# ConvGLU on one core: a looser order for the weight splits of the column tiles, and a second seven-product tile in the tenth group

## The chip, the cores and the metric

The kernel is one program on one core of a Trainium2 chip. The metric is the device time of one execution in microseconds (us); lower is better. The engines are named as in the profile: PE is the matrix engine, PEld its weight loads, DVE the vector engine, ACT the scalar engine, POOL the third elementwise engine (here it only issues DMAs), SP the queue that issues most DMAs.

## The reference, cut to what matters

A decoder block with d_model 2048 and 256 tokens: token mixers, cross-attention, and at the end a ConvGLU feed-forward of width 5632. All is float32. The change lies in the first half of the feed-forward:

```python
def conv_glu_ffn(u, w_up, conv_w, conv_b, w_down):
    gate, up = jnp.split(u @ w_up, 2, axis=-1)
    gate = causal_dwconv(gate, conv_w, conv_b)
    return (jax.nn.gelu(gate, approximate=False) * up) @ w_down
```

## The kernel before, in words

**Products in parts.** Each float32 weight tile (1 MB, 128 x 2048) is fetched by SP into a buffer named `raw` (three of them) and split into a rounded part `hi` and a remainder `lo`: ACT casts (L142), DVE subtracts (L143), in two halves of 1024 columns. `hi` and `lo` have five buffers each, so a half can only be split when the PE has let go of the half five places earlier. PE multiplies hi by hi, hi by lo and lo by hi.

**The feed-forward.** The 5632 channels are 44 chunks of 128. The first 40 go in ten groups (`FG = 10`, loop variable `p`) of four chunks. A group is eight weight tiles. An ordinary tile is 24 matmuls of 512 columns. A tile "by seven products" replaces the eight block products by seven (a Strassen-Winograd form): 21 matmuls, but DVE first makes four sums of weights (L183, 512 columns each), and the seven forms are split by ACT (L177) and DVE (L178) in three casts of 1024 columns and one of 512. `up_steps` says which tiles are so made: in groups 1 to 9 the fourth and the sixth, in group 10 the fourth alone.

The last four chunks go as eight **column tiles** (gate and up for each chunk, `for c in range(4 * FG, KF)`): a tile is 16 matmuls of 512 columns and 16 of 256, its result is joined by an ACT copy (`jt`, L290) and a DVE addition (L291). Every second column tile multiplies the `lo` halves first. After them comes the down projection, 2 x 22 tiles, of which 14 are by seven products with sums of the activations as inputs (`input_forms`, into `xs`, which the order calls `s2`).

**Work beside.** When a group's products are done, `taken_up` adds, scales and transposes the results (DVE L1227, ACT L1229, DVE L1230), POOL sends them through memory, and `four` does the convolution, gelu and product of the group's four chunks some tiles later (ACT L1189, L1164, L1184, L305; DVE L1167, L1185, L306). These steps are generators in `background`; each call of `weights()` runs one step of each and then prefetches: it issues the splits of the weight tile two ahead.

**What sets the order.** Each engine works its queue in order, and a scheduler lays the queues at build time, unless told that one instruction is to be issued after another (`issue_after`). From group 1 to the last column tile `state["strict"]` is on, and `weights()` gives two such rules: the step's instructions go after the `hi` and `lo` of the next tile, and the splits that are issued with the step go after all of the step's DVE and ACT instructions (`queued`).

Of the kernel before, what the change touches and what calls it, by code (L numbers as in the profile page):

```python
# [44 lines left out]
FG = 10  # L45


def up_steps(p):
    sevens = {3: 0, 5: 1} if p < FG - 1 else {3: 0}
    rest = [q for q in range(KD // 2) if q not in sevens.values()]  # L50
    return [(True, sevens[j]) if j in sevens else (False, rest.pop(0)) for j in range(KD // 2)]

# [20 lines left out]
def hybrid_trunk(ctx, tc, xT, memT, par, cst, msk, w_k0, w_ka, w_va, w_hg, w_hv, w_hog, w_ghg, w_bhg, w_dt,  # L73
                 w_z, w_m2, w_gm2, w_bm2, w_out, w_q, w_o, w_up, w_ut, w_dn, fin_g, outT):
    nc = tc.nc
    V, S, G, PE = nc.vector, nc.scalar, nc.gpsimd, nc.tensor
# [18 lines left out]
    order = [w_ka[n] for n in range(KD - NS)]  # L95
# [17 lines left out]
    for p in range(FG):  # L113
        for i, (seven, _) in enumerate(up_steps(p)):
            if seven:
                sums.add(len(order))
            order.append(w_up[p, i])
# [4 lines left out]
    AHEAD = 2  # L122
    WB = 5
    ready, lows = [], {}
    state = {"issued": 0, "used": 0, "strict": False}

    def halves(w, c, d, table=None):

# [69 lines left out]
    def step():  # L198
        pin.append(True)
        for gen in list(background):  # L200
            if next(gen, False) is False:
                background.remove(gen)
        pin.pop()

    def drain():
        while background:
            step()
# [5 lines left out]
    def prefetch(ahead):  # L213
        while state["issued"] < min(state["used"] + ahead, len(order)):
            issue()

    def weights():
        with ExitStack() as queued:
            if state["strict"]:
                traced = nc.cur_bb.bb.instructions  # L220
                n = len(traced)
                high, low = lows[state["used"] + 1]
                with tc.issue_after(high.ins), tc.issue_after(low.ins):
                    step()
                for ins in traced[n:]:
                    if ins.engine in (V.engine, S.engine):
                        queued.enter_context(tc.issue_after(ins))
            else:
                step()
            prefetch(1 + AHEAD)  # L230
        state["used"] += 1
        parts = ready.pop(0)
        return parts if state["used"] - 1 in sums else viewer(parts)

    def viewer(parts):
        def view(j, width):
            for a, b, hi, lo in parts:
                if a <= j * width < b:
                    o = j * width - a
                    return hi[:, o:o + width], lo[:, o:o + width]  # L240

        return view
# [22 lines left out]
    def project(hl):  # L265
        w = weights()
        ps = pj.tile([P, 512], F32, name="proj")

        mm_run(ps, w, [(k, hl[:, k, :]) for k in range(KD)], True, True, state["used"] % 2 == 0)
        return ps  # L270

    def project_tok(hl):

        ps = [pj.tile([P, 512], F32, name="proj") for _ in range(2)]
        for i in range(4):
            w = weights()
            for j in range(4):
                k = 4 * i + j
                wh, wl = w(j, 512)
                for g in range(2):  # L280
                    x1 = hl[:, k, g * P:(g + 1) * P]
                    x2 = hl[:, k, T + g * P:T + (g + 1) * P]
                    mm(ps[g], lhsT=x1, rhs=wh, start=(k == 0), stop=False)
                    mm(ps[g], lhsT=x1, rhs=wl, start=False, stop=False)
                    mm(ps[g], lhsT=x2, rhs=wh, start=False, stop=(k == KD - 1))
        return ps

    def join(pool, ps, out):
        tmp = pool.tile([P, T], F32, name="jt", bufs=2)
        S.copy(out=tmp, in_=ps[:, T:2 * T])  # L290
        V.tensor_tensor(out=out, in0=ps[:, 0:T], in1=tmp, op=ALU.add)  # L291
# [12 lines left out]
    def split(dst, src):  # L304
        S.copy(out=dst[..., 0:T], in_=src)  # L305
        V.tensor_tensor(out=dst[..., T:2 * T], in0=src, in1=dst[..., 0:T].bitcast(F32), op=ALU.subtract)  # L306
# [658 lines left out]
    for i in range(4):  # L965
        w = weights()
        ks = range(i // 2 * 8, i // 2 * 8 + 8)
        for j in range(2):
            hl_run(pss[i % 2 * 2 + j], [(*w(8 * j + k - ks[0], P), mg[:, k, :]) for k in ks],
                   i < 2, i >= 2)  # L970
# [190 lines left out]
    def convolved(c, g, taken=None):  # L1161

        gc = fu.tile([P, T], F32, name="gc", bufs=2)
        S.activation(out=gc if taken is None else token_order(gc), in_=g if taken is None else taken,  # L1164
                     func=AF.Identity, bias=pc("f_cb", c), scale=pc("f_cw", 3 * c + 2))
        for s in range(1, 3):
            V.scalar_tensor_tensor(out=gc[:, s:T], in0=g[:, 0:T - s],  # L1167
                                   scalar=pc("f_cw", 3 * c + 2 - s), in1=gc[:, s:T],
                                   op0=ALU.mult, op1=ALU.add)
        return gc  # L1170
# [62 lines left out]
        yield True  # L1233
        yield from four(p, d[0], d[1])

    state["strict"] = True
    for p in range(FG):
        acc, own = banks()
        if p % 2:
            acc, own = own, acc  # L1240
        steps = up_steps(p)
        sevens = [q for seven, q in steps if seven]
        for j, (seven, q) in enumerate(steps):
            if j % 4 == 0:
                residual_rows(2 * p + j // 4)
            w = weights()
            if seven:
                x = [up_inputs(2 * q, 0), up_inputs(2 * q + 1, 0), up_inputs(2 * q + 1, 1)] \
                    + [(xu[q][:, n, 0:P], xu[q][:, n, P:2 * P]) for n in range(4)]
                seven_products(w, x, acc, own, start=q == sevens[0], stop=q == sevens[-1])  # L1250
                if q == sevens[-1]:
                    background.append(own_later(own))
            else:
                for k in range(2):
                    for b in range(4):
                        mm_tok(acc[b], up_inputs(2 * q + k, b // 2), w(2 * k + b % 2, 512),
                               start=j == 0 and k == 0, stop=j == KD // 2 - 1 and k == 1)
        background.append(taken_up(p, acc))
    step()
    hb = big.tile([P, 8, 512], F32R, name="h")  # L1260
    hid += [hb[:, i, :] for i in range(8)]
    for c in range(4 * FG, KF):
        ps = project(u3)
        g = fu.tile([P, T], F32, name="g", bufs=1)
        join(fu, ps, g)
        V.tensor_tensor(out=g, in0=g, in1=r_f, op=ALU.mult)
        gc = convolved(c, g)
        S.activation(out=gc, in_=gc, func=AF.Gelu)
        ps = project(u3)
        up = fu.tile([P, T], F32, name="xu", bufs=1)  # L1270
        join(fu, ps, up)
        V.tensor_tensor(out=gc, in0=gc, in1=r_f, op=ALU.mult)
        V.tensor_tensor(out=gc, in0=gc, in1=up, op=ALU.mult)
        split(hid[c], gc)
    drain()
    state["strict"] = False
    fx.close()


# [158 lines left out]
def _layout(inp):  # L1438
# [25 lines left out]
    wu = wu.transpose(4, 0, 1, 3, 2, 5)  # L1464
    wu = [[x[q][[0, 1, 0, 1], [0, 1, 1, 0]] if seven else x[q].reshape(4, P, 512)
           for seven, q in up_steps(p)] for p, x in enumerate(wu)]
    wu = np.ascontiguousarray(np.array(wu).transpose(0, 1, 3, 2, 4)).reshape(FG, KD // 2, P, 2048)

# [64 lines left out]
```

## Time and profile before

| | |
|---|---|
| median of three runs | 2213.24 us (2212.03 to 2213.52) |
| the profiled execution | 2213.54 us, its span 2211.8 us |
| PE busy | 2199.7 us, 99% of the span |
| DVE busy | 1735.7 us, 78% |
| ACT busy | 1373.8 us, 62% |
| mean granted PE clock | 0.998 |

The span runs from the first to the last instruction; the execution's time is 1.7 us more. Group 9 runs from 1840.26 to 1882.42 us of the span, group 10 to 1925.26 us, the column tiles to 1974.61 us, and the down projection to the end. In the rows of a timeline the first number is the start in us, the second the duration; a bracket gives the idle time of the engine just before the row and what ended it. A group's row gives, behind the bar, the sum in us and the mean of one in ns.

### The profile page before, as it was taken

To read this page: it belongs to the slowest core of one execution; us is meant where nothing else is said; L and a number is where in the kernel's file an instruction comes from. 1 tells how busy PE (TensorE), PEld (TensorE's weight loads), DVE (VectorE), ACT (ScalarE), POOL (GpSimd) and SP (SyncE) were. 2 spreads that over 40 slices of the span, in tenths; PEclk is the share of its full clock that TensorE was granted. 3 is DMA by queue.
4 is the path that set the end of the run, shared out by engine and by line. 5 is a ranking of instruction groups with operands and counts; after the bars stand their busy time and mean duration, and the time that the engine had idled before them with its cause. 6 is when DMAs were issued, how large, how long until landed. Compare 5 with 4: busy or idle time off the path is not lost.

```text
span 2211.8 us, 32334 instructions
## 1 busy us (share of the span) xinstructions
PE 2199.7 (99%) x12151; PEld 1859.4 (84%) x12151; DVE 1735.7 (78%) x2759; ACT 1373.8 (62%) x2146; POOL 240.2 (11%) x397
## 2 busy tenths in 40 slices
PE   9999999999999999999999999999999999999998
PEld 8888888888888888888888888888888888888887
DVE  8758888887645788775677765578899999979887
ACT  7567777776545576775455655456666667655554
POOL 0100100110000122221210010010211211200000
PEclk9999999999999999999999999999999999999999
DMA  8745555555655676666675655477877777765654
GB/s 310 249 175 196 184 184 181 183 185 192 215 195 196 226 235 238 218 232 208 236 246 214 235 178 181 173 252 232 243 261 246 242 266 253 235 232 198 215 216 162
DMA packets 104285, 481.95 MB, mean 218 GB/s; under 512 B 30624, under 2 KB 35264, under 8 KB 55104
## 3 DMA queue, kind: packets, MB, share of 16 engines
q1 hardware_dynamic: 69216, 431.31, 54.9%
q0 software_dynamic: 17984, 46.16, 7.6%
q10 hardware_dynamic: 16928, 2.42, 0.6%
q8 instruction: 95, 1.56, 0.3%
q14 instruction: 62, 0.51, 0.1%
HBM read 450.96 MB, written 30.97 MB: 218 GB/s over the span
## 4 chain that ended last, share of the span: by engine, by line
PE 99%; DMA 0%; ACT 0%; DVE 0%; SPq 0%; issue 0%; DVEq 0%; ACTq 0%
PE proj L90 80%; PE misc L90 10%; PE lev L90 9%; DMA raw<-in_w_k 0%; DVE h L1385 0%; DVE raw L1387 0%; ACT lev L1386 0%; ACT hi L142 0%; PE lev L914 0%; SPq L429 0%; ACT hi L413 0%; SPq L428 0%; DVE raw L1403 0%; ACT h L305 0%; DVEq L1529 0%
## 5 line engine op out<-in xcount | busy, mean ns | idle before, releaser
L143 DVE TENSOR_TENSOR lo<-raw,hi 128x1024 fp32r<-128x1024 f32 x700 | 845.1, 1221 | 368.8 <-ACT hi L142 342.7
L142 ACT CAST hi<-raw 128x1024 fp32r<-128x1024 f32 x699 | 726.3, 1050 | 428.5 <-PE proj L90 405.5
L90 PE MATMUL proj<-hi,s 128*128 128x512 f32 x3038 | 955.9, 390 | 0.0
L90 PEld LDWEIGHTS proj<-hi,s 128*128 128x128 f32 x3038 | 570.0, 188 | 118.7 <-issue 0.7
L90 PE MATMUL proj<-lo,s 128*128 128x512 f32 x1519 | 591.4, 389 | 0.0
L90 PE MATMUL proj<-s,hi 128*128 128x512 f32 x1904 | 452.6, 392 | 3.9 <-ACT hi L142 2.8
L90 PEld LDWEIGHTS proj<-s,hi 128*128 128x128 f32 x1904 | 352.7, 189 | 74.9 <-ACT hi L142 3.4
L90 PEld LDWEIGHTS proj<-lo,s 128*128 128x128 f32 x1519 | 285.2, 188 | 58.1
L90 PEld LDWEIGHTS proj<-s,lo 128*128 128x128 f32 x1904 | 240.3, 191 | 7.7 <-issue 0.5
L90 PE MATMUL proj<-s,lo 128*128 128x256 f32 x1904 | 244.9, 283 | 0.0
L177 ACT CAST hi<-raw 128x1024 fp32r<-128x1024 f32 (+1 forms) x132 | 124.9, 946 | 122.3 <-DVE raw L183 80.0
L178 DVE TENSOR_TENSOR lo<-raw,hi 128x1024 fp32r<-128x1024 f32 (+1 forms) x132 | 141.3, 1085 | 4.7 <-ACT hi L177 4.5
L90 PE MATMUL lev<-hi,s 128*128 128x512 f32 (+1 forms) x412 | 144.4, 385 | 0.0
L90 PE MATMUL misc<-hi,s 128*128 128x512 f32 x364 | 128.9, 389 | 0.0
L339 POOL DMA_DIRECT2D x_d<-yq x120 | 69.7, 587 | 376.6 <-DVE yq L347 367.2
L183 DVE TENSOR_TENSOR raw<-raw 128x512 f32<-128x512 f32 x132 | 91.0, 690 | 3.7 <-DMA raw<-in_w_dn 0.8
L90 PEld LDWEIGHTS lev<-hi,s 128*128 128x128 f32 x412 | 76.9, 188 | 15.5
L90 PEld LDWEIGHTS misc<-hi,s 128*128 128x128 f32 x364 | 68.3, 188 | 14.2
L90 PE MATMUL lev<-lo,s 128*128 128x512 f32 (+1 forms) x206 | 79.3, 385 | 0.0
L339 POOL DMA_DIRECT2D y_d<-yq x64 | 34.8, 551 | 384.1 <-DVE sm L663 262.3
L90 PE MATMUL misc<-lo,s 128*128 128x512 f32 x182 | 70.8, 389 | 0.0
L339 POOL DMA_DIRECT2D g_d<-h x40 | 26.0, 655 | 335.8 <-DVE h L1230 335.2
(362 smaller groups left out, 2135.8 us busy)
## 6 DMA issues: line engine op xcount, KB each, us to landing
raw<-in_w_up SPq DMA_DIRECT2D x80, 1024.0 KB, 4.9
raw<-in_w_dn SPq DMA_DIRECT2D x44, 1024.0 KB, 4.8
raw<-in_w_hg SPq DMA_DIRECT2D x32, 1024.0 KB, 4.8
raw<-in_w_m SPq DMA_DIRECT2D x32, 1024.0 KB, 5.0
raw<-in_w_hv SPq DMA_DIRECT2D x16, 1024.0 KB, 4.8
raw<-in_w_hog SPq DMA_DIRECT2D x16, 1024.0 KB, 4.8
raw<-in_w_ghg SPq DMA_DIRECT2D x16, 1024.0 KB, 4.8
raw<-in_w_z SPq DMA_DIRECT2D x16, 1024.0 KB, 4.9
```

What stands on the lines that cost most here:

```text
L90: ins = PE.matmul(*args, **kwargs)
L142: high = S.copy(out=hi[:, c - a:d - a], in_=raw[:, c:d])
L143: lows[state["issued"] - 1] = high, V.tensor_tensor(out=lo[:, c - a:d - a], in0=raw[:, c:d], in1=hi[:, c - a:d - a].bitcast(F32), op=ALU.s ...
L177: high = S.copy(out=hi[:, 0:d - c], in_=raw[:, c:d])
L178: lows[state["issued"] - 1] = high, then(V.tensor_tensor(out=lo[:, 0:d - c], in0=raw[:, c:d], in1=hi[:, 0:d - c].bitcast(F32), op=ALU.subt ...
L183: then(V.tensor_tensor(out=out, in0=p, in1=q, op=op))
L339: G.dma_start(out=yd.rearrange("(n i) (b f) -> b i n f", i=B, b=P // B)[b], in_=yq[b * B:(b + 1) * B, :].rearrange("i (n f) -> i n f", n=n))
```

## The change

It has two parts. `up_steps` makes the sixth tile of group 10 by seven products too; the host lays that weight tile out to match, since the layout calls the same function. And `strict` becomes `order`, with three values: in the ten groups it is "strict" as before; in the column tiles it is "loose", where the first rule stays (a step's instructions after the next tile's `hi` and `lo`) and the second goes (splits need not wait behind the step's DVE and ACT instructions).

```diff
 def up_steps(p):
-    sevens = {3: 0, 5: 1} if p < FG - 1 else {3: 0}
+    sevens = {3: 0, 5: 1} if True else {3: 0}
...
-            if state["strict"]:
+            if state["order"]:
...
                 for ins in traced[n:]:
-                    if ins.engine in (V.engine, S.engine):
+                    if state["order"] == "strict" and ins.engine in (V.engine, S.engine):
                         queued.enter_context(tc.issue_after(ins))
...
-    state["strict"] = True
+    state["order"] = "strict"
     for p in range(FG):
...
     hid += [hb[:, i, :] for i in range(8)]
+    state["order"] = "loose"
     for c in range(4 * FG, KF):
...
     drain()
-    state["strict"] = False
+    state["order"] = None
```

The inserted line moves all later line numbers by one.

**First place: ACT in the column tiles.** `jt_18448`, `18499`, `18558`, `18619` are the join copies of the second to fifth column tiles; `hi_18516` and `hi_18520` are the two casts of the sixth tile (`raw_18514`). Before:

```order
L290 COPY jt_18499<-proj_18465 128x256
L1164 ACTIVATE gc_18503<-g_18498,par_t_77 128x256
L1268 ACTIVATE gc_18503<-gc_18503 128x256
L290 COPY jt_18558<-proj_18524 128x256
L290 COPY jt_18619<-proj_18585 128x256
L305 CAST h_18342<-gc_18399 128x256
L305 CAST h_18342<-gc_18503 128x256
L1189 COPY g_18508<-gt_18343 128x256
L1164 ACTIVATE gc_18510<-gt_18343,par_t_77 128x256
L142 CAST hi_18516<-raw_18514 128x1024
L142 CAST hi_18520<-raw_18514 128x1024
```

Now, where `jt_18508`, `18567` and `18628` are the copies of the third to fifth tiles, `hi_18525` and `hi_18529` the casts of the sixth, and `hi_18586` and `hi_18590` those of the seventh:

```order
L290 COPY jt_18508<-proj_18474 128x256
L142 CAST hi_18525<-raw_18523 128x1024
L142 CAST hi_18529<-raw_18523 128x1024
L142 CAST hi_18586<-raw_18584 128x1024
L1164 ACTIVATE gc_18512<-g_18507,par_t_77 128x256
L290 COPY jt_18567<-proj_18533 128x256
L1269 ACTIVATE gc_18512<-gc_18512 128x256
L142 CAST hi_18590<-raw_18584 128x1024
L290 COPY jt_18628<-proj_18594 128x256
```

The sixth tile's casts stood behind the join copies of the fourth and fifth tiles and the steps after them; now they stand right behind the third tile's.

**Second place: DVE from the end of group 10 to the third column tile** (`raw_18351` before, `raw_18360` now; `lo_18354` and `lo_18358`, now `lo_18363` and `lo_18367`, are its two remainders, and the second column tile's are `lo_18285` and `lo_18289`, now `lo_18294` and `lo_18298`). Before:

```order
L143 TENSOR_TENSOR lo_18289<-raw_18282,hi_18288 128x1024
L1185 TENSOR_TENSOR gc_18276<-gc_18276,vt_18026 128x256
L1227 TENSOR_TENSOR h_14637<-lev_17957,h_14637 128x512
L306 TENSOR_TENSOR s1_14633<-gc_18276,s1_14633 128x256
L1227 TENSOR_TENSOR h_14637<-misc_17959,h_14637 128x512
L1230 STREAM_TRANSPOSE h_14637<-h_14637 128x16x32 x2
L1227 TENSOR_TENSOR h_14637<-misc_17958,h_14637 128x512
L1230 STREAM_TRANSPOSE h_14637<-h_14637 128x16x32
L143 TENSOR_TENSOR lo_18354<-raw_18351,hi_18353 128x1024
L1230 STREAM_TRANSPOSE h_14637<-h_14637 128x16x32
L143 TENSOR_TENSOR lo_18358<-raw_18351,hi_18357 128x1024
```

Now:

```order
L143 TENSOR_TENSOR lo_18298<-raw_18291,hi_18297 128x1024
L1185 TENSOR_TENSOR gc_18285<-gc_18285,vt_18026 128x256
L1230 STREAM_TRANSPOSE h_14637<-h_14637 128x16x32
L1227 TENSOR_TENSOR h_14637<-misc_17959,h_14637 128x512
L306 TENSOR_TENSOR s1_14633<-gc_18285,s1_14633 128x256
L1227 TENSOR_TENSOR h_14637<-lev_17956,h_14637 128x512
L1227 TENSOR_TENSOR h_14637<-misc_17958,h_14637 128x512
L143 TENSOR_TENSOR lo_18363<-raw_18360,hi_18362 128x1024
L1230 STREAM_TRANSPOSE h_14637<-h_14637 128x16x32 x3
L143 TENSOR_TENSOR lo_18367<-raw_18360,hi_18366 128x1024
```

Three of the four transposes now stand between the two remainders of the third column tile, where one stood before; all additions L1227 still stand ahead of the first remainder.

**Third place: ACT at the first seven-product tile of the down projection** (its first inputs are the cast `s2_18811<-c_18857`, now `s2_18820<-c_18866`). Before:

```order
L1303 CAST ha_14632<-c_18857 128x128
L177 CAST hi_18904<-raw_18901 128x1024
L1300 CAST s2_18811<-c_18857 128x3x128
L177 CAST hi_18910<-raw_18901 128x1024
L177 CAST hi_18915<-raw_18901 128x1024
L177 CAST hi_18919<-raw_18901 128x512
```

Now:

```order
L177 CAST hi_18924<-raw_18910 128x1024
L305 CAST h_18351<-gc_18756 128x256
L177 CAST hi_18928<-raw_18910 128x512
L1304 CAST ha_14632<-c_18866 128x128
L142 CAST hi_18958<-raw_18956 128x1024
L1301 CAST s2_18820<-c_18866 128x3x128
```

The inputs' cast stood ahead of the tile's last three weight casts; now it stands behind all four and behind the first cast of the tile after. On PE, the scheduler has moved the products that need `s2` to the eighth matmul of this tile and later; before, the fourth was the first of them.

More of the change, by code (lines that the diff above doesn't have):

```diff
@@ L124, in hybrid_trunk @@
     ready, lows = [], {}
-    state = {"issued": 0, "used": 0, "strict": False}
+    state = {"issued": 0, "used": 0, "order": None}
     def halves(w, c, d, table=None):
```

## The prediction

> **What bounds the kernel now.** I read the page first, then what PE waited for, then the chain that ended last and the stretches around the one long wait, then the queues of ACT and DVE there. About 0.2% (4.4 us) is what a measurement of this kernel can tell from no change. The page, and PE's waits:
>
> ```profile
> span 2211.8 us, 32334 instructions
> PE 2199.7 (99%) x12151; PEld 1859.4 (84%) x12151; DVE 1735.7 (78%) x2759; ACT 1373.8 (62%) x2146; POOL 240.2 (11%) x397
> ...
> PE proj L90 <- ACT hi L142: 2.8, 1, 2.8
> PE proj L90 <- ACT hi L413: 1.1, 3, 0.6
> ```
>
> PE bounds everything, so only what PE does or waits for counts: one wait of 2.8 us for a split, and three small ones at the start of the kernel, which the change does not touch. The chain places the wait, and gives PE's pace:
>
> ```profile
> 1587.46 16.32 PE proj L90 x72
> ...
> 1925.42 27.81 PE proj L90 x160
> ...
> 1955.06 0.94 ACT hi L142
> ...
> 1956.05 18.56 PE proj L90 x96
> ```
>
> The first row is 72 matmuls of 512 columns: 16.32 / 72 = 0.2267 us each. The second is five column tiles of 32 matmuls: 27.81 / 5 = 5.562 us a tile. Then PE stands until the sixth tile's cast. The last row is the three remaining column tiles: at the same pace they would take 3 x 5.562 = 16.69 us, but they take 18.56, which is 1.87 us more. The stretches say why (columns: stretch, its length, busy us and instructions of PE, PEld, DVE, ACT and POOL, granted PE clock, DMA share, GB/s):
>
> ```profile
> 1840.26:1882.42 42.16, 42.16 (x188) 34.91 (x186) 41.03 (x57) 28.37 (x42) 7.99 (x12) 1.00 0.74 250
> 1882.42:1925.26 42.84, 42.84 (x191) 35.47 (x189) 38.88 (x55) 29.62 (x44) 8.00 (x12) 1.00 0.79 270
> 1925.26:1953.20 27.94, 27.94 (x161) 24.42 (x159) 19.32 (x31) 12.16 (x19) 8.00 (x12) 1.00 0.70 226
> 1953.20:1956.05 2.85, 0.01 (x2) 0.00 (x1) 1.68 (x5) 2.80 (x7) 0.00 (x0) 1.00 0.00 0
> ...
> 1957.33:1960.74 3.41, 3.41 (x10) 2.64 (x9) 3.38 (x7) 2.71 (x5) 0.00 (x0) 0.50 0.36 89
> ```
>
> Just behind the wait PE runs at a granted clock of 0.50 for 3.41 us (mean over the whole run: 0.998, so there is hardly another such stretch). Half of 3.41 is 1.71 us, and with a few slow starts that is the 1.87. So the wait costs 2.80 + 1.87 = 4.67 us, not 2.80. Short waits at the start do not bring this on:
>
> ```profile
> 10.60 0.74 PE L90 MATMUL proj<-s,hi 128*128 128x512 f32 x2 [0.63 <-ACT hi L413]
> ...
> 12.00:16.00 4.00, 4.00 (x25) 3.53 (x24) 4.00 (x9) 4.00 (x10) 0.00 (x0) 1.00 1.04 423
> ```
>
> **Why PE waits there.** ACT's queue, and the fetch of the sixth tile:
>
> ```profile
> 1942.14 0.37 ACT L290 COPY jt<-proj 128x256 f32<-128x256 f32 x1 [0.76 <-PE proj L90]
> ...
> 1947.68 0.37 ACT L290 COPY jt<-proj 128x256 f32<-128x256 f32 x1 [2.06 <-PE proj L90]
> 1953.25 0.37 ACT L290 COPY jt<-proj 128x256 f32<-128x256 f32 x1 [5.20 <-PE proj L90]
> 1953.54 0.71 ACT L305 CAST h<-gc 128x256 fp32r<-128x256 f32 x2
> ...
> 1954.46 0.60 ACT L1164 ACTIVATE gc<-gt,par_t 128x256 f32<-128x256 f32 x1
> 1954.97 1.98 ACT L142 CAST hi<-raw 128x1024 fp32r<-128x1024 f32 x2
> ...
> 1934.88 0.33 SPq L156 DMA_DIRECT2D raw<-in_w_ut  x1
> ```
>
> The fetch is issued at 1934.88, twenty us ahead of the cast, so data are not what is late. ACT idles 5.20 us at the join copy of the fifth tile, which needs the fifth tile's end; the casts that PE needs to go on from there stand behind it.
>
> **The change, step by step.**
>
> *Loose order.* The sixth tile's casts now stand right behind the join copy of the third tile (1942.14 here). The first needs the `hi` buffer of the third tile's second half, five places earlier, which is free by then; the second that of the fourth tile's first half, some 2 us on. With 1 us each both are done about 8 us before PE wants them at 1953.2. Gain: 2.80 us of wait and the 1.87 us behind it. It is 4.67 whole or nearly nothing, since the half-clock stretch hangs on the wait.
>
> *Seven products in the tenth group.* PE: 24 - 21 = 3 matmuls less, 3 x 0.2267 = 0.68 us. DVE and ACT get more work:
>
> ```profile
> L143 DVE TENSOR_TENSOR lo<-raw,hi 128x1024 fp32r<-128x1024 f32 x700 | 845.1, 1221 | 368.8 <-ACT hi L142 342.7 <-PE proj L90 20.7 <-issue 1.8
> L142 ACT CAST hi<-raw 128x1024 fp32r<-128x1024 f32 x699 | 726.3, 1050 | 428.5 <-PE proj L90 405.5 <-PE misc L90 9.1 <-issue 5.3
> ...
> L178 DVE TENSOR_TENSOR lo<-raw,hi 128x1024 fp32r<-128x1024 f32 x99 | 120.6, 1219 | 0.6 <-ACT hi L177 0.3
> L177 ACT CAST hi<-raw 128x1024 fp32r<-128x1024 f32 x99 | 104.3, 1054 | 89.6 <-DVE raw L183 61.1 <-PE misc L90 14.2 <-PE proj L90 6.2
> L183 DVE TENSOR_TENSOR raw<-raw 128x512 f32<-128x512 f32 x132 | 91.0, 690 | 3.7 <-DMA raw<-in_w_dn 0.8
> L178 DVE TENSOR_TENSOR lo<-raw,hi 128x512 fp32r<-128x512 f32 x33 | 22.6, 686 | 4.1 <-ACT hi L177 4.1
> L177 ACT CAST hi<-raw 128x512 fp32r<-128x512 f32 x33 | 20.6, 623 | 32.7 <-DVE raw L183 18.9 <-PE misc L90 9.9 <-PE proj L90 3.9
> ```
>
> DVE: 4 x 0.690 + 3 x 1.219 + 0.686 - 2 x 1.221 = 4.66 us more; ACT: 3 x 1.054 + 0.623 - 2 x 1.050 = 1.69 us more. ACT has 13 us free in the group (29.62 of 42.84). DVE is tighter, but group 9 already has two such tiles: 41.03 of 42.16 us busy, and PE has no wait in it. The tenth group then looks like the ninth, and what DVE leaves over goes into the column tiles, where it idles 27.94 - 19.32 = 8.6 us.
>
> *Where that cover is thin.* Behind the group DVE must finish the third column tile's second remainder in time. The same work behind group 9 is in the trace; PE's first matmul of group 10 and of the column tiles, and DVE's remainders of the third tile in each:
>
> ```profile
> 1882.42 0.39 PE L90 MATMUL lev<-hi,s 128*128 128x512 f32 x1
> 1891.95 2.36 DVE L143 TENSOR_TENSOR lo<-raw,hi 128x1024 fp32r<-128x1024 f32 x2 [0.23 <-ACT hi L142]
> ...
> 1925.26 0.52 PE L90 MATMUL proj<-s,lo 128*128 128x256 f32 x3
> 1933.63 1.18 DVE L143 TENSOR_TENSOR lo<-raw,hi 128x1024 fp32r<-128x1024 f32 x1
> ```
>
> Behind a group with two such tiles the second remainder ends 1894.31 - 1882.42 = 11.89 us after the group; now, in the column tiles, it ends at 9.55. The third column tile takes `lo` first and reaches its second half after two tiles and eight matmuls of 256 columns, (5.562 - 16 x 0.2267) / 16 = 0.121 us each: 2 x 5.562 + 0.97 = 12.09 us. Margin before 2.5 us, after the change 0.2. Cost 0; bounds: no gain is possible, and at worst all 4.66 us and the 0.68 by which PE is earlier fall ahead of it, 9.55 + 0.68 + 4.66 - 12.09 = 2.80 us. I take 0, by group 9, whose queue it nearly copies.
>
> *First seven-product tile of the down projection.* Its inputs' cast now stands behind the first cast of the next tile, which must wait for the `hi` buffer of the tile before. That is free when that tile's last matmul ends, 0.39 - 0.23 = 0.16 us into the seven-product tile; with 1.05 for the cast and the inputs' cast
>
> ```profile
> 1994.41 0.51 ACT L1300 CAST s<-c 128x384 fp32r<-128x384 f32 x1
> ```
>
> the inputs are there after 0.16 + 1.05 + 0.51 = 1.72 us. The scheduler has put seven matmuls ahead of the first that needs them, 1.59 us. Cost 0.1 us; bounds 0 and 0.5 (as if ACT took one more 0.37 us copy between).
>
> *Queues passed.* SP issues a raw tile when DVE has made its last remainder; the sixth column tile's fetch moves about 11.89 - 9.55 - 0.68 = 1.7 us later, to 1936.5, and PE needs that tile at 1953.2 - 0.68 = 1952.5. POOL's issues keep their order; the two loads of residual rows and the one of `gr` move by an issue or two in the down projection, and nobody reads them soon. The tenth group's own sums come two tiles later and are read only at its end.
>
> **Sum.** -2.80 - 1.87 - 0.68 + 0 + 0.1 = -5.25 us. The profiled execution took 2213.54 us (span 2211.8 and 1.7 around it), 0.3 above the median: it would take 2208.3, and the median 2213.24 - 5.25 = 2208.0 us, -0.24%.
>
> **A rule against the trace.** The half clock is where a rule would move the sum. The Trainium skill, "TensorE: Matmul & The Clock Gate", section "HAM oscillation — how this bites in real kernels", says that PE must not idle for more than about 3.4 us, and that the clock is halved behind such a gap. By it a gap of 2.80 us would not halve the clock; the 1.87 us would then have another cause and stay. The trace does not agree: the gap is 2.80 us, and the only half-clock stretch after the start lies 1.3 us behind it. The page's window of 3413 ns agrees with the 3.41 us of the stretch.
>
> **Rivals.**
>
> (1) *The half-clock stretch does not hang on the wait.* Then only 2.80 + 0.68 - 0.1 = 3.38 come back: 2209.9 us, within 0.2%. For it: 2.80 us is not long, and the fastest of the three runs is 1.2 us below the median, as if some runs had no such stretch. Against it: 0.50 stands there and the mean is 0.998. The page's rule above leads to this time. Chance 0.08.
>
> (2) *DVE is late at the third column tile by up to 2.80 us.* A middle value of 1 us gives 2209.0; with 2.80 and a new half-clock stretch, 2208.0 + 4.67 = 2212.7. For it: the margin is 0.2 us, and three transposes stand between the tile's two remainders. Against it: group 9. Chance 0.12.
>
> (3) *The loose order does not free the splits*, because buffers hold them: 2213.24 - 0.68 + 0.1 = 2212.7. Against it: PE lets the buffers go tile by tile, and ACT idles 2.06 and 5.20 us there. Chance 0.03.
>
> (4) *Slower.* At the same place DVE is late by all 2.80 us, and the scalings between its additions and transposes wait too:
>
> ```profile
> 1890.25 0.72 ACT L1229 ACTIVATE h<-h,r_fc 128x512 f32<-128x512 f32 x1 [0.47 <-DVE h L1227]
> ```
>
> Four such waits are 4 x 0.47 = 1.88 us, since three scalings now stand behind a join copy on ACT. 2.80 + 1.88 + 1.87 = 6.55 us of new wait and half clock eat the 5.25 and more: 2214.5. It decides from a wait of 5.25 - 1.87 = 3.4 us. Chance 0.03, half of it for over 0.2%.
>
> **Numbers.** The forecast has 0.74. Its own range is 2207.0 to 2209.0, by the runs' spread of 1.5 us and a term of up to 0.9 at the third tile. Since 0.2% ends at 2208.8, about 0.69 of the 0.74 falls under it, and 0.03 of rival (2): faster 0.72. Within: 0.05 + 0.08 + 0.09 + 0.03 and 0.015 of (4), 0.265. Slower: 0.015. The range takes in rivals (1) and the smaller half of (2): 2207.0 to 2210.6.
>
> **What the profile after would show.** PE's waits without the row of 2.8 us on the split; a granted clock of 1.00 from group 10 to the down projection; eight column tiles in 8 x 5.56 = 44.5 us; the sixth tile's first cast some 8 us or more ahead of its first matmul; the tenth group in 42.16 us. A PE wait on a `lo` of DVE in the third column tile means rival (2), and 0.1 to 0.5 us on ACT's input cast in the fifth down tile the small term. If a stretch at 0.50 stands elsewhere, rival (1) was right; if the long wait is still there, rival (3). The forecast is wrong if DVE cannot take the 4.66 us.

## The result, and the profile after

The kernel after takes 2208.77 us (median of 17 runs, 2208.0 to 2210.02), the kernel before 2213.52 us in the same session (17 runs, 2212.03 to 2215.62). The ratio is 0.9979, 95% interval 0.9973 to 0.9986: 4.75 us or 0.21% faster. The forecast was 2208.0 us, its range 2207.0 to 2210.6. The profiled execution after took 2208.0 us, its span 2206.2.

The page's first line, and the view of what PE waited for (us in total, times, longest):

```profile
span 2206.2 us, 32339 instructions
PE 2197.6 (100%) x12148; PEld 1858.1 (84%) x12148; DVE 1739.0 (79%) x2765; ACT 1374.9 (62%) x2148; POOL 240.2 (11%) x397
...
PE misc L90 <- POOL eps_t L370: 1.0, 1, 1.0
PE proj L90 <- ACT hi L413: 0.4, 2, 0.3
```

PE has 3 matmuls fewer (12148 against 12151). The wait of 2.8 us on a split of L142 is gone; what is left lies at the start of the kernel. The chain in the column tiles:

```profile
1922.95 1.36 PE misc L90 x6
1924.31 44.45 PE proj L90 x256
1968.75 1.39 PE lev L90 x6
```

Before, this stood there as two rows of PE with ACT's cast between them; now all eight tiles are one piece, 44.45 / 8 = 5.556 us a tile. The stretches of group 9 (to within 0.2 us), of group 10, of the column tiles, and of the time at which PE stood and then ran at half clock before:

```profile
1840.00:1882.16 42.16, 42.16 (x187) 34.91 (x187) 41.03 (x57) 28.39 (x42) 7.99 (x12) 1.00 0.75 250
...
1881.98:1924.14 42.16, 42.16 (x187) 34.91 (x186) 41.02 (x57) 28.41 (x42) 8.00 (x12) 1.00 0.75 249
1924.14:1968.59 44.45, 44.45 (x257) 39.36 (x256) 35.38 (x53) 29.63 (x46) 8.00 (x12) 1.00 0.75 261
...
1954.00:1958.00 4.00, 4.00 (x29) 3.73 (x28) 1.93 (x3) 2.32 (x3) 0.00 (x0) 1.00 0.68 245
```

The granted clock (the eighth column from the left, behind POOL) is 1.00 in each of them. Group 10 takes the 42.16 us of group 9, with DVE as busy as there (41.02 against 41.03).

What ACT and DVE do at the two places that the forecast spoke of, and the one place where PE stumbles now (timelines):

```profile
1941.02 0.37 ACT L290 COPY jt<-proj 128x256 f32<-128x256 f32 x1 [0.39 <-PE proj L90]
1942.06 2.00 ACT L142 CAST hi<-raw 128x1024 fp32r<-128x1024 f32 x2 [0.67 <-DMA raw<-in_w_ut]
...
1931.03 1.22 DVE L143 TENSOR_TENSOR lo<-raw,hi 128x1024 fp32r<-128x1024 f32 x1
1932.16 1.89 DVE L1230 STREAM_TRANSPOSE h<-h 128x512 f32<-128x512 f32 x3
1933.97 1.18 DVE L143 TENSOR_TENSOR lo<-raw,hi 128x1024 fp32r<-128x1024 f32 x1
...
1991.74 0.39 PE L90 MATMUL lev<-hi,ha 128*128 128x512 f32 x1
1992.09 0.50 PE L90 MATMUL lev<-hi,s 128*128 128x512 f32 x1
1992.43 0.39 PE L90 MATMUL lev<-lo,s 128*128 128x512 f32 x1
1992.66 0.40 PE L90 MATMUL lev<-lo,ha 128*128 128x512 f32 x1
...
1991.53 0.51 ACT L1301 CAST s<-c 128x384 fp32r<-128x384 f32 x1
```

The sixth tile's two casts are done at 1944.06; PE comes to that tile at 1924.14 + 5 x 5.556 = 1951.92. By the bracket the first of them waited 0.67 us for the fetch of its tile: what holds these casts now is the data, and no longer their place in ACT's queue. DVE ends the third tile's second remainder at 1935.15, which is 11.0 us behind the start of the column tiles, and PE needs it at 12.09. In the fifth down tile the two starts 1991.74 to 1992.09 and 1992.09 to 1992.43 are 0.35 and 0.34 us apart where a matmul takes 0.227: a stall of 0.24 us. Its first half is the wait for the inputs' cast, which ends at 1991.53 + 0.51 = 1992.04.

### The profile page after: what moved, and what is told of

It is laid out like the page before. It is cut to its first block, busy times and chain, and to the rows that moved or that the text cites. A ratio compares the mean times of both kernels' runs of the same rounds, so it can differ in the third digit from the quotient of the medians.

```text
span 2206.2 us, 32339 instructions
## 1 busy us (share of the span) xinstructions
PE 2197.6 (100%) x12148; PEld 1858.1 (84%) x12148; DVE 1739.0 (79%) x2765; ACT 1374.9 (62%) x2148; POOL 240.2 (11%) x397
## 4 chain that ended last, share of the span: by engine, by line
PE 99%; DMA 0%; DVE 0%; ACT 0%; SPq 0%; issue 0%; DVEq 0%; ACTq 0%
PE proj L90 80%; PE misc L90 10%; PE lev L90 9%; DMA raw<-in_w_k 0%; DVE h L1386 0%; DVE raw L1388 0%; ACT lev L1387 0%; PE lev L914 0%; SPq L429 0%; ACT hi L413 0%; SPq L428 0%; DVE raw L1404 0%; DVEq L1530 0%; ACT r L1397 0%; DVE raw L1407 0%
## 5 line engine op out<-in xcount | busy, mean ns | idle before, releaser
L142 ACT CAST hi<-raw 128x1024 fp32r<-128x1024 f32 x697 | 724.4, 1050 | 433.0 <-PE proj L90 406.9
```

Source lines behind the costliest of these rows:

```text
L142: high = S.copy(out=hi[:, c - a:d - a], in_=raw[:, c:d])
```

## The experiments

I split the profiled span in three, at two of PE's rows that every kernel has: its first matmul of group 10 and its first of the column tiles. All in us; the times of PE's rows are from the timelines.

```
kernel                      group 10 starts   group 10 takes   from the column tiles to the end
before                      1882.42           42.84            286.52
after                       1881.98           42.16            282.10
loose order only            1881.94           42.84            281.80
second seven tile only      1882.41           42.16            285.17
before, wait filled         1882.24           42.84            285.15
loose order in the groups   1882.35           42.16            281.80
```

The first column moves by up to 0.48 us and knows nothing of the edits (on PE, the first five kernels are the same up to there): that is the start of the kernel, which differs between executions. The other two are exact to some 0.02 us.

**Each part alone.** `e1_loose_only` is the kernel after with the tenth group as before:

```
-    sevens = {3: 0, 5: 1} if True else {3: 0}
+    sevens = {3: 0, 5: 1} if p < FG - 1 else {3: 0}
```

> Only the first part of the change: the column tiles' splits are free, the tenth group keeps one tile by seven products. Theory A (the wait on the sixth column tile's split and the half-clock stretch behind it go together): 2.80 + 1.87 = 4.67 us less than before, -0.21%, no PE row for hi in the eight column tiles, no stretch at half clock, and no stall in the down projection (its inputs' cast comes as late as before). Theory B (the half clock comes whatever the wait): 2.80 us less, -0.13%, and a stretch of some 3.4 us at 0.5 in or behind the column tiles. Theory C (the gain of the change comes from the second seven-product tile): within 0.5 us of before.

Measured: 2208.84 us (11 runs) against 2213.45 (30 runs of the kernel before, shared with `e2_seven_only`, `e3_filled` and `e6_loose_groups`), ratio 0.9981, 0.9972 to 0.999. From the column tiles on it takes 286.52 - 281.80 = 4.72 us less. In its chain the column tiles are one piece, and the down projection has no stall:

```profile
1924.94 44.45 PE proj L90 x256
```

As far as this run goes theory A holds; B and C fall. `e2_seven_only` is the kernel before with the line `sevens = {3: 0, 5: 1}` for every group.

> Only the second part: the tenth group has two tiles by seven products, the column tiles keep the strict order of before. Theory A: 3 matmuls x 0.2267 = 0.68 us less than before, -0.03%; the wait of about 2.8 us on hi at the sixth column tile and 3.4 us at half clock right behind it are still there. Theory C (the gain comes from this part): 3 to 5 us less, the wait gone or much shorter. A small loss of up to 0.3 us in the down projection may come with it, if the stall seen after the change belongs to this part.

Measured: 2213.03 us (11 runs), ratio 0.9996, 0.9987 to 1.0004. Group 10 takes 0.68 us less, as expected, and the wait is there:

```profile
PE proj L90 <- ACT hi L142: 2.8, 1, 2.8
...
1955.36 0.98 PE L90 MATMUL proj<-s,hi 128*128 128x512 f32 x3 [2.84 <-ACT hi L142]
...
1950.27:1953.69 3.42, 2.25 (x10) 1.52 (x9) 0.40 (x2) 1.13 (x4) 0.00 (x0) 1.00 0.20 75
1953.69:1957.10 3.41, 1.74 (x7) 1.42 (x8) 3.02 (x6) 3.41 (x7) 0.00 (x0) 1.00 0.00 0
1957.10:1960.51 3.41, 3.41 (x22) 3.03 (x21) 3.38 (x7) 2.71 (x5) 0.00 (x0) 1.00 0.48 151
```

But no half clock follows: 1.00 in all three stretches, and 22 matmuls in the last where the kernel before had 10. From the start of the last matmul ahead of it to the start of the next, less one matmul's 0.227 us, PE stood for 3.00 us in both kernels (the brackets, here 2.84, count from the modelled end of that last matmul, 0.16 us later). The same wait brought the half clock in the one execution and not in the other. So theory A in its plain form (wait and half clock go together) is wrong, though the first experiment bore it out.

**The wait filled.** `e3_filled`:

```
+        if c == 4 * FG + 2:
+            fill = pm_.tile([P, 512], F32, name="misc")
+            for _ in range(12):
+                tc.keep_in_program_order(PE.matmul(fill, lhsT=u3[:, 0, 0:P], rhs=u3[:, 1, :], start=True, stop=True))
```

> The kernel before with 12 matmuls of 512 columns whose result nobody reads, put on PE just ahead of the sixth column tile, where PE waits 2.80 us: 12 x 0.2267 = 2.72 us of work in the place of the wait. The wait's end doesn't move, PE is busy until it. Theory A (PE's idling brings the half clock): no stretch at 0.5 in the column tiles, 1.87 us less than before, -0.08%; if the 12 take a little more than the wait, 1.5 to 1.9 us less. Theory B (half clock whatever PE does there): the stretch stays, within 0.4 us of before.

Measured: 2212.15 us (11 runs), ratio 0.9995, 0.9986 to 1.0004, which cannot tell 1.87 us from nothing. The trace can: 285.15 against 286.52, and 1.00 throughout.

```profile
1952.87 2.88 PE L1272 MATMUL misc<-s 128*128 128x512 f32 x12
1955.88 0.50 PE L90 MATMUL proj<-s,hi 128*128 128x512 f32 x1
...
1953.48:1956.89 3.41, 3.29 (x15) 2.40 (x14) 2.69 (x5) 3.41 (x7) 0.00 (x0) 1.00 0.00 0
1956.90:1960.31 3.41, 3.41 (x19) 2.91 (x18) 3.37 (x8) 2.72 (x6) 0.00 (x0) 1.00 0.28 62
```

The sixth tile starts no earlier than its split allows, and the kernel still ends 1.37 us sooner. After the second experiment one such trace alone is no proof; the next runs say what it is worth.

**Waits of chosen length.** In the kernel after, ACT casts a piece of the fifth column tile several times over, and PE reads the last copy ahead of the sixth tile in one matmul whose result nobody uses (n is 1, 3 and 4; `gap_4e` has n = 4 two tiles earlier). The edit, without the two lines that also hold the column tiles' matmuls in the program's order:

```
+        if c == 4 * FG + 2:
+            probe = pm_.tile([P, 512], F32, name="misc")
+            link = fu.tile([P, 192], F32R, name="link")
+            for _ in range(n):
+                tc.keep_in_program_order(S.copy(out=link, in_=ps[:, T:T + 192]))
+            mm(probe[:, 0:192], lhsT=u3[:, 0, 0:P], rhs=link, start=True, stop=True)
```

> The kernel after with a wait of chosen length put on PE between the fifth and the sixth column tile: one small cast of a finished tile on ACT, and one matmul of 192 columns on PE that reads it and whose result nobody uses. Here one cast, an idle PE of about 0.7 us. Theory A1 (the length of the idle stretch decides on the half clock, with a threshold between 0.7 and 2.8 us): no stretch at half clock, 0.7 to 1.0 us over after. Theory A2 (any idle stretch at this place brings it): 3.4 us at 0.5, 1.7 us more.

> As the one before with three casts: an idle PE of about 2.3 us. Nothing in the traces so far says on which side of a threshold this is. With a half-clock stretch about 2.3 + 1.7 = 4.0 us over after, without one 2.3 us.

> As the one before with four casts: an idle PE of about 2.8 us, the length of the wait that the kernel before has. Theory A1 or A2: about 3.4 us at 0.5, beginning one to two us behind the end of the wait, and 2.8 + 1.7 = 4.5 us over after. If the half clock of the kernel before came from something else (theory B), 2.8 us over after and the clock at 1.0 throughout.

> The same wait of about 2.8 us, 11.1 us (two column tiles) earlier. If only the length counts: the same half-clock stretch, as far behind the end of the wait as in the one before. If the place in some fixed beat counts too: another distance, or no half clock at all.

One execution each: 2209.66, 2211.90, 2211.93 and 2214.63 us. PE stood for 0.57, 2.09, 2.44 and 3.89 us (counted as above), and behind the last three, not the first, the clock fell. Theory A2 falls. The stretches of `gap_3` and `gap_4e`:

```profile
1951.15:1954.56 3.41, 1.49 (x8) 0.95 (x7) 2.67 (x4) 2.56 (x6) 0.00 (x0) 1.00 0.79 255
1954.57:1957.98 3.41, 3.41 (x10) 2.67 (x10) 0.34 (x1) 0.00 (x0) 0.00 (x0) 0.50 0.71 286
...
1940.01:1943.41 3.40, 1.33 (x6) 0.75 (x4) 2.98 (x5) 1.65 (x4) 0.00 (x0) 1.00 0.99 368
1943.42:1946.83 3.41, 1.76 (x5) 1.47 (x6) 2.04 (x3) 2.39 (x6) 1.43 (x2) 0.50 1.02 418
1946.83:1950.24 3.41, 3.41 (x10) 2.64 (x9) 0.97 (x2) 1.15 (x3) 1.41 (x2) 0.50 0.86 316
```

In `gap_3` a wait of 2.09 us, shorter than the 3.00 us that left the clock alone above, halves it. In `gap_4e` PE still stands when the clock falls at 1943.42. So it isn't the length, and theory A1 falls too. Every stretch at full speed in these traces lasts a whole number of times 3.4133 us (572 of them in the kernel before from 4.90 to 1957.33 us, 645 in `e2_seven_only`, 644 in the kernel after): the clock changes only on a beat. Where the beat lies against the program differs: its first change comes between 4.5 and 7.1 us. Each stretch of 3.4 us quoted is one beat. That makes theory P: after a beat in which PE was idle for too long the next is at half clock, however long the wait around it.

**Several waits in one run**, each elsewhere in the beat: the same lines behind every column tile. PE stood at six, six and five of the eight places; at the last ones it had matmuls of the down projection to do.

> The kernel after with such a wait behind each of the eight column tiles, two casts each, an idle PE of some 1.3 to 1.9 us each time; each wait falls elsewhere in the 3.413 us beat in which the clock changed so far. Theory P (half clock follows when PE is idle in one beat for more than a bound between 1.68 and 2.08 us): no half clock, 8 to 15 us over after. Theory L (any wait of 2 us and more brings it, wherever it falls): none either, apart from waits that come out at 2 us. Both fall if half clock follows waits of 1.5 us.

> As the one before with three casts each, some 2.0 to 2.4 us. Theory P: half clock only behind waits that lie nearly whole in one beat; waits that a beat's end cuts into parts below 1.68 us leave the clock at 1.0. So a share of the eight, the others not; and each change of the clock comes at a beat's end. Theory L: half clock behind all that are longer than 2.1 us.

> As the one before with five casts each, some 2.6 to 3.0 us, as long as the wait of the kernel before. Theory P: half clock behind most of them (where the beat's end leaves more than 2.08 us in one beat), none where it cuts the wait in the middle. Theory L: behind all of them.

One execution each: 2222.36, 2229.94 and 2232.71 us. The first wait of each run came out at 3.6 to 4.6 us, since DVE or ACT was late there. The waits of 2.14 us in `gaps8_3` and of 1.97 us in `gaps8_5`, each with the beats around it:

```profile
1953.30 0.36 PE L90 MATMUL misc<-link,s 128*128 128x192 f32 x1 [1.98 <-ACT link L1267]
1948.22:1951.63 3.41, 3.10 (x14) 2.24 (x12) 0.99 (x1) 1.27 (x2) 0.17 (x1) 1.00 0.99 358
1951.63:1955.04 3.41, 1.74 (x8) 1.48 (x9) 2.21 (x4) 2.14 (x6) 0.00 (x0) 1.00 0.64 204
1955.04:1958.46 3.42, 3.42 (x22) 3.02 (x21) 1.52 (x4) 2.74 (x4) 0.00 (x0) 1.00 0.29 120
...
1943.90 0.36 PE L90 MATMUL misc<-link,s 128*128 128x192 f32 x1 [1.81 <-ACT link L1267]
1941.55:1944.96 3.41, 1.60 (x14) 1.40 (x13) 2.75 (x4) 1.87 (x6) 0.91 (x2) 1.00 0.79 238
1944.97:1948.37 3.40, 3.40 (x15) 3.11 (x14) 0.07 (x1) 0.00 (x0) 1.92 (x3) 0.50 1.00 387
```

The longer wait, cut by a beat's end into 0.47 and 1.67 us, leaves the clock at 1.00; the shorter, whole in one beat, halves it. `gaps8_5` has a second wait of the same 1.81 us in the bracket, at 1963.39, which a beat's end at 1962.03 cuts: 2.05 us of busy PE behind that end, and the clock stays at 1.00. Theory L falls, P holds. Over all traces, inside the kernel, the next beat was at half clock after PE was busy for 1.60 us or less of the 3.41 (0.16 to 1.60, eleven beats), and at full clock from 1.74 up. At half clock, beats with 1.76 to 2.86 us of busy PE brought no return; those with 3.15 us and more did. `gaps8_2` did have a half clock, which theory P's text excluded, because its first wait came out at 3.56 us where 1.9 was meant; its other waits, up to 1.79 us, left the clock alone.

The rule explains the pair that broke theory A. Busy time in the beats around the wait: 2.25 and 1.74 us in `e2_seven_only` (above), and in the kernel before

```profile
1950.50:1953.91 3.41, 2.71 (x12) 1.89 (x11) 0.00 (x0) 0.66 (x3) 0.00 (x0) 1.00 0.01 5
1953.91:1957.33 3.42, 1.28 (x6) 1.06 (x7) 2.96 (x6) 3.42 (x8) 0.00 (x0) 1.00 0.00 0
```

The same wait of 3.00 us, cut in the middle there and near its start here. In `e3_filled` a beat ends at 1953.48, so that unfilled the wait would have had 2.40 of its 3.01 us in one beat: by the rule it is the filling that kept the clock up.

**The loose order in the groups too**, `e6_loose_groups`, in the search for a better kernel:

```
-    state["order"] = "strict"
+    state["order"] = "loose"
```

> The kernel after with the loose order in the ten groups too, where it has the strict one. Of the strict order nothing is left. In the trace after, PE waits in this stage for nothing longer than 0.3 us, so there is little to gain: theory A expects 2.0 us at most either way against after, so 2.5 to 6.5 us less than before, most likely about 5. Theory D (the strict order is what keeps the groups' splits in time): the splits drift behind the background work of the groups, PE waits for hi or lo in several groups, and 5 us or more go lost against after.

Measured: 2207.91 us (8 runs, 2207.61 to 2208.18), ratio to before 0.9975, 0.9965 to 0.9985. Its waits of PE, all in the first 10 us of the kernel or so:

```profile
PE misc L90 <- POOL eps_t L370: 1.0, 1, 1.0
PE proj L90 <- ACT hi L413: 0.5, 1, 0.5
PE proj L90 <- DVE lb L500: 0.2, 1, 0.2
```

Theory D falls, and the stall of the fifth down tile is gone (281.80 against 282.10). It is the fastest version, though its interval overlaps that of the kernel after; 0.30 us of the 0.86 between the medians is seen in the traces, the rest is not explained.

## Why the prediction was right, and where not

By the traces the change is worth 0.68 us in group 10, 4.72 us in the column tiles (loose order alone, against an execution with a half-clock beat), and costs 282.10 - 281.80 = 0.30 us in the down projection: 5.10 us. Another 0.44 us of the 5.54 between the two profiled executions lies ahead of group 10. The medians cannot tell these terms apart: 0.9973 to 0.9986 is 3.1 to 6.0 us.

- *The wait, -2.80.* Right. It is gone with the loose order alone and stands with the second part alone. The casts were done 7.9 us ahead of PE, where about 8 were forecast; but it was the fetch that held them, not the buffers that the forecast named, so that the two agree so well is in part luck.
- *The half clock, -1.87.* The mechanism was half right, the size a little too big. It hangs on the wait, and rival (1) (it comes anyway) is refuted: no half clock in any trace without a long wait, the start and the end of the kernel apart. But "the 1.87 us behind it" was taken as certain, from one execution, and "4.67 whole or nearly nothing" is wrong: `e2_seven_only` and `e3_filled` lack the half clock and keep the late split. A wait of 3.00 us leaves less than 1.60 to 1.74 us of busy PE in some beat only for part of the positions. With 1.68 to 1.81 us of idle time as the bound, that part is (3.41 - 3.00 + 2 x (3.00 - 1.81 to 1.68)) / 3.41 = 0.82 to 0.89, if all positions are equally likely. The beat itself is worth 1.54 us here (286.52 - 285.17 = 1.35, and 0.19 for a stall that `e2_seven_only` has at the start of the down projection, where PE comes sooner: two of its matmuls there start 82 and 110 ns late). The rest of the 1.87 belongs to the wait: by the starts of PE's rows it is 3.00 us, not 2.80, and from the sixth tile to the down projection takes 18.39 us before, 16.84 in `e2_seven_only` and 16.67 for three tiles without a wait, so 0.17 us of slower starts come with a wait at full clock too. 3.00 + 0.17 + 1.55 are the 4.72. With the share of positions, the mean price of the half clock is estimated at some 1.3 us, and 5.10 becomes about 4.9; 4.75 was measured, and the interval above takes in both.
- *Group 10, -0.68.* Exact: 42.84 to 42.16 us. Between the medians of runs it does not show: `e1_loose_only` without it is 0.07 us from the kernel after. Less the 0.30 us of stall named below, it is worth 0.38 us by the traces.
- *Third column tile, 0.* Right. The margin is 12.09 - 11.0 = 1.1 us where group 9 gave 0.2; rivals (2) and (4) did not come near.
- *First seven-product tile of the down projection, +0.1.* Right place, 0.24 us by the rows and 0.30 by the span, within the bounds of 0 and 0.5. The wait itself is the 0.12 us between the first two rows, near the 0.1 that was summed; the slower starts behind it were not in the sum. It belongs to the two parts together: the loose order alone has no stall, and the strict order dropped from the groups takes it away.
- *Rival (3)*, the order frees nothing: refuted by the first experiment. What the rule that the loose order keeps is worth is not shown: no run has the column tiles without any order.

The rule weighed in the prediction, of the Trainium skill ("TensorE: Matmul & The Clock Gate", section "HAM oscillation — how this bites in real kernels"), that PE must not idle for more than about 3.4 us, is too lenient for these runs: 1.97 us inside a beat halved the clock. What the same page says in "Part 1: The HAM clock gate", that the window of 3413 ns runs freely, agrees with the beats above.

## What to carry to other kernels

Price a wait of PE by where it can fall in a beat of 3.41 us, not by its length alone: below some 1.7 us here it cost itself, from 2 us on it could cost another 1.5 us or so, in some executions and not in others, and in the one trace with the wait filled by idle matmuls that part was not paid. One profiled execution shows one position of the beat, so look at whether the half clock is in the trace before it goes into a sum as certain. And where an order is forced so that one stage's splits come in time, let go of it where the stage's work is of another shape: an in-order ACT put a cast behind a copy that waited for PE, and PE then waited for the cast. Try the looser order elsewhere too: the groups did not need the strict one.

## What the runs showed of the hardware

- The PE clock changes only on a beat of 3.4133 us; a beat with PE busy for 1.60 us or less (47%) was followed by half clock, one with 1.74 us or more (51%) was not, in all thirteen traces (the busy time has modelled ends, so the bound is known to about 0.1 us).
- The way back takes more: beats at half clock with 1.76, 2.26, 2.30 and 2.86 us of busy PE were followed by another at half clock, one with 3.15 us was not.
- The beat starts elsewhere in each execution (first full speed at 4.5 to 7.1 us). By the rule the kernel before should then have executions with and without its 1.5 us. The mean clock, rounded to three places, shows part of it: 0.998 or less in 9 of 30 executions of the kernel before and 4 of 11 of `e2_seven_only`, in none of 47 of the four kernels in which PE does not stand ahead of the sixth column tile (after, `e1_loose_only`, `e3_filled`, `e6_loose_groups`). `gap_3` and `gap_4`, each with one beat at half clock, show 0.999 too, so the share of such executions is estimated above and not counted.
